# The first products of a decoder layer: two weights loaded in quarters, their products taken by inner tile in two banks, x loaded on GpSimd's queue, eight constant products in front instead of fourteen

## The chip, the core and the metric

The kernel runs on one core of a Trainium2 chip. The metric is the device time of one execution in microseconds; the time before is the median of three runs. The engines are named as the profile names them: PE is TensorE (matrix products), ACT is ScalarE, DVE is VectorE, POOL is GpSimd, SP is SyncE, which here only issues DMA transfers. PE, ACT, DVE, POOL and SP each work through their own instructions in a fixed order and wait on semaphores for one another. ACT, POOL and SP can each issue transfers; each has its own queue.

## The reference

One decoder layer on x, 1024 tokens by 1024 features, in float32: a SwiGLU feed-forward, a mixer (stick-breaking attention beside a Mamba-2 scan), cross-attention to 256 memory tokens, and a second SwiGLU, each between RMS norms. The change touches only the start of the first feed-forward:

```python
f = swiglu(rmsnorm(h, ffn1_pre_g[l]), ffn1_w_gu[l], ffn1_w_down[l])
h = h + 0.5 * rmsnorm(f, ffn1_post_g[l])

def swiglu(h, w_gu, w_down):
    gu = h @ w_gu
    g, u = jnp.split(gu, 2, axis=-1)
    return (jax.nn.silu(g) * u) @ w_down
```

The hidden width is 2816, 22 column tiles of 128 for the gate `g` and 22 for `u`.

## The kernel before

**Layout.** x is held transposed, features on the 128 partitions: 8 inner tiles (`d` or `k`, 0 to 7), each for two halves `hh` of the sequence, 512 tokens wide. An inner tile of one half is 128 x 512 floats, 256 KB. A weight tile is one column tile of 128 with all its 8 inner tiles, 128 x 8 x 128 floats, 512 KB.

**Precision.** Each float32 operand is split into a high part (rounded, by ScalarE) and a low part (the difference, by VectorE): `split` for weights (`whi`, `wlo`, from `wraw`), `scaled_split` for x times its gain (`xh`, `xl`, from the tiles `S`, which serve as landing place of x at the beginning). `mm3` then issues three products for one inner tile: high x high, high weight x low x, low weight x high x. So one column tile for one half takes 8 x 3 = 24 products of 512 columns, accumulated in one PSUM bank.

**The norm.** The products are made on x times gain, without the norm's factor. The factor of each token is found beside them: squares on ScalarE, sums on VectorE (`sumsq`, tile `acc`), a small product with ones (`rms_cols`, 4 products of one column, tile `ms`), root and reciprocal (`cpre`), and 4 products with the identity that lay the factor out as a row (`rms_rows`), copied to `rpre`. `gate` multiplies a finished bank by `rpre` and takes SiLU (tile `ft`); `up` multiplies the result by the other bank. Until `rpre` is there, a bank cannot be freed. Tag `mm` has three banks, tag `dn` four.

**The first stage.** `up_phase` begins with constant products (`warm`: ones x ones into `ms`, the result is not used). Then for weights 0, 1, 2 (gate 0, up 0, gate 1) it makes the weight tile (`wtile`: load, split) and after each calls `begin(i)`: x of half 0, then constants and the norm of half 0, then x and norm of half 1. The products follow in the order gate 0, up 0, gate 1 on half 0, then the same on half 1, then the weights 3, 4, 5 from a stream. The first three column tiles (`f` = 0 to 2) are done so; from f = 3 on (`seven`) the products run in a seven-product scheme on combined blocks, whose sums are made on VectorE and GpSimd (`wc`, `sq`, `e`, `S`).

**What sets the order.** TensorE's order is the order of the program: each product is tied behind the one before (`_pe`). A clock of estimated costs is kept beside (`self.clock`); `pinned(t)` places the norm's small products behind the first product at which that clock passes `t`. The other engines' orders come from a scheduler, except for instructions under `kp` while `inlater` holds, which keep the program's order, and `urgent`, which raises a priority. In the first two steps `inlater` holds. A pool's tag with `bufs=n` has n slots; the next tile of the tag waits until the oldest is free: `wraw` has 2 (each 512 KB of weight), `whi` and `wlo` 3 each, `raw2` 2.

## Time and profile before

| | us |
|---|---|
| median of 3 runs | 2595.53 |
| lowest, highest | 2594.32, 2598.31 |
| profiled execution, its own time | 2597.14 |
| span of that execution | 2595.4 |
| busy in the span: PE, DVE, ACT, POOL | 2573.2, 1989.8, 1290.5, 575.4 |

How to read the rows: a timeline row has start and duration in us, the engine, the line of the program, the operation, the tiles written and read (buffer numbers left out), the shape and the number of instructions merged into the row; in brackets the time that the engine sat idle before, and what ended it. `SPq` and `POOL DMA_DIRECT2D` rows are the issue of a transfer, not the transfer. A row of the DMA view names a transfer, its size and the time from issue to landing. A row by form gives the duration of one in ns as minimum, median and maximum. Products overlap in TensorE, so a product's duration is longer than the step from one to the next; the pace is read from starts.

### The profile page before, as it was taken

The page shows a single profiled execution, that of the slowest core. Times are in us where ns is not written, and L with a number is a line of the kernel's source. Part 1 is how long each engine was busy: PE and PEld are TensorE (multiplying, and loading weights), DVE is VectorE, ACT ScalarE, POOL GpSimd, SP SyncE. Part 2 cuts the span into 40 slices and gives each one's busy share as a digit, 9 for nine tenths or more (in the row PEclk, how much of TensorE's full clock was granted, in tenths as well). Part 3 has the DMA queues.
Part 4 walks back from the last instruction along what each step waited for, and adds up shares of the span by engine and source line. Part 5 has one row for each costly group of instructions (what it writes and reads, how often), then busy time and mean ns, then how long its engine had stood idle before and what let it go on. Part 6 is the DMA issues. An engine that isn't in the chain of part 4 may idle for free.

```text
span 2595.4 us, 36790 instructions
## 1 busy us (share of the span) xinstructions
PE 2573.2 (99%) x12850; PEld 2148.3 (83%) x12850; DVE 1989.8 (77%) x3049; ACT 1290.5 (50%) x2301; POOL 575.4 (22%) x668
## 2 busy tenths in 40 slices
PE   9999999999999999999999999999999999999999
PEld 7888888887787888888888898888878888888887
DVE  7888997779689884777777777876656888767767
ACT  7434444555356663555555554445554433334544
POOL 2555553001000001111111110101011655542000
PEclk9999999999999999999999999999999999999999
DMA  6448888655565516555554556547658453327554
GB/s 244 157 178 296 307 291 312 206 184 178 216 209 193 183 70 226 160 150 145 150 155 131 157 173 206 206 162 251 202 179 304 143 179 102 112 84 239 183 175 154
DMA packets 216042, 489.82 MB, mean 189 GB/s; under 512 B 26544, under 2 KB 35120, under 8 KB 215856
## 3 DMA queue, kind: packets, MB, share of 16 engines
q1 hardware_dynamic: 169232, 381.02, 45.0%
q0 software_dynamic: 22720, 62.93, 8.1%
q10 hardware_dynamic: 23904, 43.53, 4.5%
q8 instruction: 101, 1.65, 0.3%
q14 instruction: 85, 0.70, 0.1%
HBM read 327.46 MB, written 138.94 MB: 180 GB/s over the span
## 4 chain that ended last, share of the span: by engine, by line
PE 88%; DVE 4%; issue 1%; DMA 1%; ACT 1%; POOL 0%; DVEq 0%; ACTq 0%; POOLq 0%
PE mm L139 46%; PE dn L139 33%; PE z L139 2%; PE tr L142 2%; PE ms L142 1%; PE y L139 1%; PE ms L139 1%; PE seg L139 1%; PE st L139 0%; DVE wlo L263 0%; DMA wraw<-xs 0%; DVE hl L263 0%; DMA oraw<-mix 0%; PE mm L142 0%; DMA raw<-xs 0%
## 5 line engine op out<-in xcount | busy, mean ns | idle before, releaser
L139 PE MATMUL mm<-xh,whi 128*128 128x512 f32 x1312 | 519.7, 405 | 2.0 <-ACT sq L1806 1.4
L139 PE MATMUL mm<-xh,wlo 128*128 128x512 f32 x1280 | 491.5, 392 | 0.0
L139 PE MATMUL mm<-xl,whi 128*128 128x512 f32 (+1 forms) x1248 | 485.2, 389 | 0.3 <-DVE xl L270 0.3
L139 PEld LDWEIGHTS mm<-xh,wlo 128*128 128x128 f32 x1280 | 240.3, 188 | 52.4 <-DVE wlo L263 0.4
L139 PEld LDWEIGHTS mm<-xh,whi 128*128 128x128 f32 x1312 | 246.8, 188 | 44.1 <-issue 3.9
L139 PEld LDWEIGHTS mm<-xl,whi 128*128 128x128 f32 x1248 | 235.4, 189 | 34.1 <-DVE xl L270 1.0
L1792 DVE TENSOR_TENSOR_SCAN nb<-nb,begin 128x128 f32<-128x128 f32 (+7 forms) x128 | 171.5, 1351 | 41.9 <-ACT nb L1788 40.7
L1788 ACT ACTIVATE nb<-z,scale 128x128 f32<-128x128 f32 (+2 forms) x192 | 108.2, 580 | 70.7 <-PE z L139 70.2
L263 DVE TENSOR_TENSOR wlo<-wraw,whi 128x1024 fp32r<-128x1024 f32 x70 | 85.4, 1220 | 51.6 <-ACT whi L261 48.2
L261 ACT CAST whi<-wraw 128x1024 fp32r<-128x1024 f32 (+1 forms) x86 | 83.5, 970 | 73.8 <-PE mm L139 51.7
L1809 POOL DMA_DIRECT2D mix<-sq x64 | 52.8, 825 | 251.0 <-DVE sq L1807 190.5
L658 ACT ACTIVATE ft<-ft 128x512 f32<-128x512 f32 x88 | 55.5, 632 | 95.4 <-DVE ft L657 94.8
L139 PE MATMUL dn<-xh,wlo 128*128 128x512 f32 x296 | 101.2, 389 | 0.0
L761 POOL TENSOR_TENSOR wc<-raw,wraw 128x512 f32<-128x512 f32 x55 | 81.1, 1474 | 56.0 <-DVE wlo L263 23.3
L263 DVE TENSOR_TENSOR atl<-tr,ath 128x512 fp32r<-128x512 f32 (+1 forms) x107 | 67.3, 630 | 32.2 <-ACT ath L261 31.8
L761 POOL TENSOR_TENSOR wc<-wraw,raw 128x512 f32<-128x512 f32 x56 | 78.6, 1404 | 52.2 <-DVE whi L263 16.5
L261 ACT CAST ath<-tr 128x512 fp32r<-128x512 f32 (+1 forms) x107 | 58.3, 545 | 58.8 <-PE tr L142 55.6
L858 POOL TENSOR_TENSOR ft<-ft,e 128x512 f32<-128x512 f32 x37 | 59.8, 1616 | 124.4 <-DVE e L854 56.5
L139 PE MATMUL mm<-ath,v 128*128 128x256 f32 x320 | 84.6, 287 | 0.7 <-ACT sq L1806 0.5
L139 PE MATMUL dn<-xh,blk 128*128 128x512 f32 x264 | 85.2, 389 | 0.0
L139 PE MATMUL mm<-atl,v 128*128 128x256 f32 x320 | 83.1, 282 | 0.7 <-DVE atl L263 0.7
L261 ACT CAST wlo<-wc 128x512 fp32r<-128x512 f32 x79 | 49.1, 621 | 68.6 <-PE dn L139 22.1
(582 smaller groups left out, 6770.9 us busy)
## 6 DMA issues: line engine op xcount, KB each, us to landing
whi<-dwhi SPq DMA_DIRECT2D x82, 512.0 KB, 3.7
wlo<-dwlo SPq DMA_DIRECT2D x82, 512.0 KB, 5.0
wraw<-in_w_gu SPq DMA_DIRECT2D x43, 512.0 KB, 4.2
dwhi<-bh SPq DMA_DIRECT2D x78, 256.0 KB, 4.1
dwlo<-bl SPq DMA_DIRECT2D x78, 256.0 KB, 4.0
raw<-in_w_gu SPq DMA_DIRECT2D x37, 512.0 KB, 4.1
wraw<-xs SPq DMA_DIRECT2D x56, 256.0 KB, 3.0
xs<-ft ACTq DMA_DIRECT2D x54, 256.0 KB, 3.0
```

Source lines behind the costliest of these rows:

```text
L139: self._pe(self.nc.tensor.matmul(out, lhsT, rhs, start=start, stop=stop, skip_group_check=self.more), cost)
L142: self._pe(self.nc.tensor.transpose(out, src, self.ident if ident is None else ident), 109.0)
L261: self.kp(self.nc.scalar.copy(hi, src))
L263: self.nc.vector.tensor_tensor(out=lo, in0=src, in1=hi.bitcast(F32), op=ALU.subtract)
L658: nc.scalar.activation(t, t, AF.Silu)
L761: inst = (nc.vector if early else nc.gpsimd).tensor_tensor(out=t, in0=a, in1=b, op=op)
L858: nc.gpsimd.tensor_tensor(out=t1, in0=t1, in1=e, op=ALU.mult)
L1788: nc.scalar.activation(nb[:, s0:s1], z[:, 0:n], AF.Sigmoid, scale=sc[:, i : i + 1])
L1792: nc.vector.tensor_tensor_scan(out=nb[:, 0:Wd][:, ::-1], data0=nb[:, 0:Wd][:, ::-1], data1=begin[:, S - Wd : S][:, ::-1], initial=0.0, op0 ...
L1809: nc.gpsimd.dma_start(out=self.mix_d[p][a * 64 : a * 64 + 64, csl], in_=o, accum_op=ALU.add)
```

## The change

Weights 0 and 1 get their landing tiles and split tiles at once, and each is loaded in four transfers, two inner tiles (128 KB) each, alternating between the two weights, on SP's queue. Tile 0 of x for half 0 follows the first quarter on the same queue; the other 15 tiles of x (both halves) are issued on GpSimd's queue, where before four were. The parameters are issued on ScalarE's queue, not on SP's. The splits of the quarters stand between those of x in the program's order. Weight 2 lands in a slot of `raw2` instead of `wraw`. The products of weights 0 and 1 on half 0 run side by side: for each inner tile three products of the one into one bank, three of the other into a second, both of tag `dn` (before: all of weight 0 into a bank of `mm`, then all of weight 1). The norm's small products of half 0 are pinned at 17500 and 21000 instead of 8500 and 13500; those of half 1 stay at 24000 and 27500. `warm` makes 8 constant products instead of 14.

```diff
-            first = []
-            begin(-1)
-            for i in range(3):
-                self.inlater = i < 2
-                first.append(self.wtile(wgu[i]))
-                begin(i)
-                self.inlater = False
+            begin.warm()
+            first, raws = [], []
+            for i in range(2):
+                raws.append(self.t(self.wp, [P, KT, P], F32, "wraw", bufs=2))
+                first.append([self.t(self.wp, [P, KT, P], F32R, n, bufs=3) for n in ("whi", "wlo")])
+            quarters = [(i, slice(2 * n, 2 * n + 2)) for n in range(4) for i in range(2)]
+            for n, (i, q) in enumerate(quarters):
+                self.tc.keep_in_program_order(nc.sync.dma_start(out=raws[i][:, q], in_=wgu[i][:, q]))
+                if n == 0:
+                    begin.load(0, 0, nc.sync)
+            for d in range(1, 2 * KT):
+                begin.load(d // KT, d % KT, nc.gpsimd)
+            self.inlater = True
+            for n, (i, q) in enumerate(quarters):
+                self.split(*(x[:, q] for x in first[i]), raws[i][:, q])
+                if n < 2:
+                    begin.split(0, n)
+                elif n % 2:
+                    begin.split(0, n - 1)
+                    begin.split(0, n)
+            begin.behind()
+            raw = self.t(rw, [P, KT, P], F32, "raw2", bufs=2)
+            self.tc.keep_in_program_order(nc.sync.dma_start(out=raw, in_=wgu[2]))
+            first.append([self.t(self.wp, [P, KT, P], F32R, n, bufs=3) for n in ("whi", "wlo")])
+            self.split(*first[2], raw)
+            begin.consts()
+            begin.norm(0, 17500, 21000)
+            self.inlater = False
+            for d in range(KT):
+                begin.split(1, d)
+            begin.norm(1, 24000, 27500)
...
-            ts = []
-            for hh in range(2):
-                up(0, hh, gate(first[0], hh), first[1])
-                ts.append(gate(first[2], hh))
+            ps = [self.t(self.dnp, [P, H], F32, "dn", bufs=4) for _ in range(2)]
+            for k in range(KT):
+                for (wh, wl), x in zip(first, ps):
+                    self.mm3(x, [(wh[:, k, :], wl[:, k, :], self.XH[0][k], self.XL[0][k])], k == 0, k == KT - 1)
+            t = ft()
+            with self.urgent():
+                scaled(t, ps[0], 0)
+                nc.vector.tensor_tensor(out=t, in0=t, in1=ps[1], op=ALU.mult)
+            store(0, 0, t)
+            ts = [gate(first[2], 0)]
+            up(0, 1, gate(first[0], 1), first[1])
+            ts.append(gate(first[2], 1))
...
-            nc.sync.dma_start(out=self.params, in_=ap["params"])
+            nc.scalar.dma_start(out=self.params, in_=ap["params"])
...
-                for _ in range(14):
+                for _ in range(8):
```

Three places show how the instructions move. First TensorE's beginning; `whi_215` and `whi_246` are weights 0 and 1 before, `whi_208` and `whi_211` after, `xh_4` and `xh_5` the high parts of inner tiles 0 and 1. Before:

```order
L139 MATMUL ms_198<-onesr_115 128x512 x14
L139 MATMUL mm_376<-xh_4_80,whi_215 128x512
L139 MATMUL mm_376<-xl_20_96,whi_215 128x512
L139 MATMUL mm_376<-xh_4_80,wlo_216 128x512
L139 MATMUL mm_376<-xh_5_81,whi_215 128x512
L139 MATMUL mm_376<-xl_21_97,whi_215 128x512
```

and with the change:

```order
L140 MATMUL ms_198<-onesr_115 128x512 x8
L140 MATMUL dn_388<-xh_4_80,whi_208 128x512
L140 MATMUL dn_388<-xl_20_96,whi_208 128x512
L140 MATMUL dn_388<-xh_4_80,wlo_209 128x512
L140 MATMUL dn_389<-xh_4_80,whi_211 128x512
L140 MATMUL dn_389<-xl_20_96,whi_211 128x512
L140 MATMUL dn_389<-xh_4_80,wlo_212 128x512
L140 MATMUL dn_388<-xh_5_81,whi_208 128x512
```

Each inner tile of x now feeds six products instead of three before the next tile is asked for, and both weights are needed from the start.

Second, ScalarE around the two norms; `sq_105` to `sq_111` are squares of half 1, `whi_675` is the fourth weight (its slot is weight 0's), `rpre_101` the factor of half 0. With the change:

```order
L335 ACTIVATE cpre_100_305<-ms_307,small_114 128x4
L360 ACTIVATE acc_104_336<-S_73_189 128x512
L363 ACTIVATE sq_107_344<-S_74_190 128x512
L363 ACTIVATE sq_108_347<-S_75_191 128x512
L363 ACTIVATE sq_109_350<-S_75_191 128x512
L262 CAST whi_675<-wraw_673 128x1024
L363 ACTIVATE sq_110_353<-S_76_192 128x512
L350 COPY rpre_101_306<-ms_314 128x512
L363 ACTIVATE sq_111_356<-S_76_192 128x512
```

Before, the fourth weight's CAST stood 13 instructions behind the row's copy; now it stands two ahead of it.

Third, VectorE in the first of the seven-product tiles (f = 3), where `e_184` gathers a difference of products and the other rows are low parts of weights and of x. Before:

```order
L730 SCALAR_TENSOR_TENSOR cb_892<-cb_892,params_78,cb_893 128x512
L263 TENSOR_TENSOR xl_28_104<-braw_815,xh_12_88 128x512
L263 TENSOR_TENSOR wlo_976<-wc_974,wlo_976 128x512
L827 TENSOR_TENSOR e_184<-sq_270_950,dn_998 128x512
L263 TENSOR_TENSOR xl_29_105<-rpost_835,xh_13_89 128x512
```

and with the change:

```order
L755 SCALAR_TENSOR_TENSOR cb_904<-cb_904,params_78,cb_905 128x512
L264 TENSOR_TENSOR xl_28_104<-braw_827,xh_12_88 128x512
L852 TENSOR_TENSOR e_184<-sq_270_962,dn_1010 128x512
L264 TENSOR_TENSOR wlo_988<-wc_986,wlo_988 128x512
L264 TENSOR_TENSOR xl_29_105<-rpost_847,xh_13_89 128x512
```

The difference `e` now goes one place earlier, ahead of a weight's low part. From about the second seven-product tile (f = 4) on, the order on every engine is the same as before.

More of the change, by code (lines that the diff above doesn't have):

```diff
@@ L1 @@
 from contextlib import ExitStack, contextmanager
+from types import SimpleNamespace
 import numpy as np
@@ L2273, in consts, with load_x, split_x, behind @@
                     nc.vector.tensor_scalar(out=g, in0=g, scalar1=0.5, scalar2=None, op0=ALU.mult)
-            def load_x(hh):
-                order = self.tc.keep_in_program_order
-                for d in range(KT):
-                    x, eng = self.F[hh][d], (nc.sync, nc.gpsimd)[d % 2 if hh == 0 else 0]
-                    order(eng.dma_start(out=x, in_=ap["xT"][d, :, hh * H : (hh + 1) * H]))
-                    self.scaled_split(self.XH[hh][d], self.XL[hh][d], x, self.par("ffn1_pre_g", d))
-                if hh == 0:
-                    order(nc.gpsimd.tensor_copy(small[:, 4:5], self.XH[0][6][:, 0:1].bitcast(F32)))
+            order = self.tc.keep_in_program_order
+            def load_x(hh, d, eng):
+                order(eng.dma_start(out=self.F[hh][d], in_=ap["xT"][d, :, hh * H : (hh + 1) * H]))
+            def split_x(hh, d):
+                self.scaled_split(self.XH[hh][d], self.XL[hh][d], self.F[hh][d], self.par("ffn1_pre_g", d))
+            def behind():
+                order(nc.gpsimd.tensor_copy(small[:, 4:5], self.XH[0][6][:, 0:1].bitcast(F32)))
             def warm():
@@ L2296, in norm_x @@
                 self.pre(hh, accs, t1, t2)
-            def begin(step):
-                if step < 0:
-                    warm()
-                elif step == 0:
-                    load_x(0)
-                elif step == 1:
-                    consts()
-                    norm_x(0, 8500, 13500)
-                else:
-                    load_x(1)
-                    norm_x(1, 24000, 27500)
+            begin = SimpleNamespace(
+                warm=warm, load=load_x, split=split_x, behind=behind, consts=consts, norm=norm_x,
+            )
             self.kv_d = [[tc.dram_tile([P, 4, MEM], F32R, name=f"kv{h}{n}") for n in range(2)] for h in range(4)]
```

## The prediction

> **What bounds the kernel now.** First the page, busy time by engine.
>
> ```profile
> PE 2573.2 (99%) x12850; PEld 2148.3 (83%) x12850; DVE 1989.8 (77%) x3049; ACT 1290.5 (50%) x2301; POOL 575.4 (22%) x668
> ```
>
> TensorE is busy for 2573.2 of 2595.4 us: only 22 us in the whole kernel are idle. So the second view is TensorE's timeline of the beginning (start and duration in us, in brackets the idle time before and what ended it), with a line of the chain for the pace of undisturbed products. The page counts the constant products `ms<-onesr` as work; here they are part of the loss.
>
> ```profile
> 1.10 6.18 PE L139 MATMUL ms<-onesr 128*128 128x512 f32 x14 [1.10 <-POOL onesr L2265]
> 7.50 0.50 PE L139 MATMUL mm<-xh,whi 128*128 128x512 f32 x1 [0.22 <-ACT xh L268]
> 8.29 0.50 PE L139 MATMUL mm<-xl,whi 128*128 128x512 f32 x1 [0.30 <-DVE xl L270]
> ...
> 23.21 1.02 PE L139 MATMUL ms<-small,acc 128*128 128x1 f32 x8 [0.22 <-DVE acc L363]
> 24.09 0.48 PE L139 MATMUL mm<-xh,wlo 128*128 128x512 f32 x1
> ...
> 25.57 1.06 PE L139 MATMUL ms<-ident,cpre 128*128 128x128 f32 x8
> 26.38 0.47 PE L139 MATMUL mm<-xh,wlo 128*128 128x512 f32 x1
> ...
> 28.02 0.50 PE L139 MATMUL mm<-xh,whi 128*128 128x512 f32 x1 [0.47 <-DVE ft L657]
> 116.22 2.72 PE dn L139 x12
> ```
>
> An undisturbed product takes 2.72 / 12 = 0.2267 us. The first useful one starts at 7.50, and the first one on the second half of the sequence (hh = 1) at 28.02. Between them lie 72 products (3 weights x 8 inner tiles x 3), 16.32 us, and the small products of the first norm, (24.09 - 23.21) + (26.38 - 25.57) = 1.69 us. The rest, 28.02 - 7.50 - 16.32 - 1.69 = 2.51 us, is lost in waits. Without the norm, which moves, the second half starts at 28.02 - 1.69 = **26.33 us**: that is the number to beat. From there on TensorE is full up to 90 us (stretches: length, then busy time of each engine), so what is won by then is kept at least so far.
>
> ```profile
> 28.00:52.00 24.00, 23.98 (x113) 20.11 (x114) 17.55 (x26) 17.31 (x25) 2.12 (x4) 1.00 0.35 122
> 52.00:90.00 38.00, 38.00 (x168) 31.16 (x166) 31.71 (x42) 23.45 (x40) 19.66 (x27) 1.00 0.68 228
> ```
>
> **The first product.** Before, it waits for tile 0 of x, which stands on SP's queue behind 512 KB of weight.
>
> ```profile
> 1.19 0.42 SPq L185 DMA_DIRECT2D wraw<-in_w_gu  x1
> 1.66 2.10 SPq L2279 DMA_DIRECT2D S<-in_xT  x4
> wraw<-in_w_gu SPq DMA_DIRECT2D x1, 512.0 KB, 4.1
> S<-in_xT SPq DMA_DIRECT2D x1, 256.0 KB, 5.0
> 6.72 2.56 ACT L268 ACTIVATE xh<-S,params 128x512 fp32r<-128x512 f32 x4 [0.40 <-DMA S<-in_xT]
> 7.50 2.73 DVE L270 SCALAR_TENSOR_TENSOR xl<-S,params,xh 128x512 fp32r<-128x512 f32 x4
> 0.00:2.00 2.00, 1.00 0.11 18
> 2.00:3.00 1.00, 1.00 0.96 190
> 3.00:4.00 1.00, 1.00 0.96 324
> 4.00:5.00 1.00, 1.00 0.98 354
> 5.00:6.00 1.00, 1.00 1.00 332
> 6.00:7.00 1.00, 1.00 1.03 375
> 7.00:8.00 1.00, 1.00 1.04 416
> 8.00:9.00 1.00, 1.00 1.03 404
> 9.00:10.00 1.00, 1.00 1.06 395
> ```
>
> The last rows are stretches: length, granted clock, DMA share, GB/s. Tile 0 landed at 1.66 + 5.0 = 6.66 us, and the first product followed 0.84 us later. Adding the rates up, 1.48 MB had moved by 6.66; parameters, weight and tile 0 are 0.89 MB of that, so GpSimd's tiles beside them multiplied the wait by 1.66. Now only parameters, a quarter weight and tile 0 stand ahead, 0.50 MB. Alone they would be down at 3.9 us; with as much again on GpSimd's queue at 5.3; at the measured 1.66, 0.83 MB, at 4.8 us. I take 4.8: the first product starts at 4.8 + 0.84 = **5.64 us**, the second, behind the subtraction on VectorE, another 0.79 later (8.29 - 7.50), at **6.43**.
>
> **The 71 products from there** take 16.1 us at full pace, to 22.5 us, if three supplies keep up. *Data:* per inner tile TensorE needs 6 x 0.2267 = 1.36 us. At 38% of the traffic (0.66 / 1.66 = 40% is the most that GpSimd's queue can have had before) tile 4 lands at 9.8 us, its two parts are ready 0.7 + 0.7 us later, at 11.3, and the products ask for them from 11.6 on; tile 5 is ready at 13.0 and asked for at 13.0; tiles 6 and 7 have more room, because SP's queue runs dry at about 11.3 (2.07 MB at 62%). The parameters on ScalarE's queue cost it an issue ahead of its first table load, at a time when it has nothing to do: free. *Splitting:* the quarters cost more instructions.
>
> ```profile
> L261 ACT CAST whi<-wraw x6: 1038/1042/1055, 5.3 to 46.5; 128x1024 fp32r<-128x1024 f32 x6
> L263 DVE TENSOR_TENSOR wlo<-wraw,whi x6: 1218/1224/1225, 6.4 to 47.7; 128x1024 fp32r<-128x1024 f32 x6
> L261 ACT CAST blk<-wraw x1: 618/618/618, 55.7 to 55.7; 128x512 fp32r<-128x512 f32 x1
> L263 DVE TENSOR_TENSOR blk<-wraw,blk x1: 685/685/685, 56.4 to 56.4; 128x512 fp32r<-128x512 f32 x1
> ```
>
> Carrying the step from 1024 to 512 elements on to 256 gives 0.41 us on ScalarE and 0.42 on VectorE. Two inner tiles need 2 x (0.41 + 0.64) = 2.1 us on ScalarE (2.56 / 4 for x) and 2 x (0.42 + 0.68) = 2.2 on VectorE (2.73 / 4), under TensorE's 2.72: hidden. The third weight lands near 11.3, its split ends by 15.6, and it is first asked for at 17.1. *Pace:* this is the term that decides.
>
> ```profile
> L139 PE MATMUL ms<-onesr x7: 470/628/628, 4.2 to 6.8; 128*128 128x512 f32 x7
> ```
>
> The fourteen constant products run at (6.8 - 1.1) / 13 = 0.438 us each, half pace, though the granted clock stands at 1.00; only the last is shorter (0.470), and the useful ones are fast. So it took about 5.7 us of products to reach full pace. Eight of them last 3.5 us, to 4.6; then TensorE sits for 1 us. What is left to run slowly I bound from both sides: 14 - 8 = 6 products if the break costs nothing, 14 if it starts the count afresh. Each slow product costs 0.438 - 0.227 = 0.211 us. I take the middle, ten, 2.1 us, since the break is of the size neither to be ignored nor to count as a stop; that also gives the tiles 4 to 7 room. The second half then starts at 22.5 + 2.1 = **24.6 us** (23.8 to 25.5). Gain: 26.33 - 24.6 = **1.7 us** (0.8 to 2.5).
>
> [...]
>
> **What follows.** The inputs of the second half land by about 21 us (7 MB in all at the rates above) and are needed from 24.6 on. The first norm now sits at the 81st product; on VectorE a split of 1.2, seven sums and four splits of x at about 0.67 each stand before it from 14.4 on, so its sum is ready near 23 us and asked for at 26.6: free. The second norm is tight. ScalarE takes the fourth weight's CAST ahead of the first norm's row copy, and that CAST waits until product 96 frees its slot. Behind it: 1.04 on ScalarE, then on VectorE 1.1 for the split, two scalings and two sums at about 0.6 each: 4.7 us. TensorE has 19 products and a norm's row, 19 x 0.2267 + 0.81 = 5.1 us less the tail of product 96, 4.9. I cost it at nothing; if late, at most 1 us. The third weight sits in a `raw2` slot, so one of GpSimd's later loads of x (L674) waits for its split near 15.6; in ScalarE's order the first use of these loads comes behind the first norm's row and SiLU, ten microseconds and more later: free. The three banks of `mm` hold, because the first two products now lie in `dn`: the wait of 0.47 us at 28.02 is part of the 2.51 us that go.
>
> Further on only VectorE's order moves, and there the first of two waits is met:
>
> ```profile
> 90.32 3.00 PE L139 MATMUL dn<-S,whi 128*128 128x512 f32 x12 [0.30 <-DVE e L827]
> ...
> 113.21 3.01 PE L139 MATMUL mm<-S,wlo 128*128 128x512 f32 x12 [0.85 <-DVE e L827]
> ```
>
> The difference `e` now goes ahead of a split of 0.685 us, so this 0.3 us should go. The 0.85 us wait before 113 us hangs on GpSimd's chain, whose order is unchanged: kept.
>
> **Sum:** 1.7 + 0.3 = 2.0 us. The profiled execution took 2597.14 us (span 2595.4 and 1.7 around it), 1.6 above the median of the runs, 2595.53. So 2595.1 for such an execution and **2593.5 us** for the median.
>
> **Rivals.**
> *Full pace at once* (0.18). Against it stand the thirteen slow products; for it, that products were fast at 8.29 right after a 0.2 us wait. Then the second half starts at 22.5: gain 3.8 + 0.3 = 4.1, **2591.4 us**.
> *The gain is given back* (0.20). For it: POOL's chain and the waits at 90 and 113 us, and later phases that wait for DMA; against: every later order is unchanged and TensorE drives it. Then **2595.5**, within the runs' own 4 us.
> *Slower: the quarters arrive late* (0.08). The 128 KB of constants took 7.9 us to land in the traffic and the 105 KB of parameters 2.1 almost alone:
>
> ```profile
> rpost<-in_consts SPq DMA_DIRECT2D x1, 128.0 KB, 7.9
> params<-in_params SPq DMA_DIRECT2D x1, 105.0 KB, 2.1
> ```
>
> If a quarter cannot go faster than 128 / 105 x 2.1 = 2.6 us and they do not overlap, the last pair lands at about 2 + 8 x 2.6 + 0.7 (tile 0) = 23.5 us; with 1.4 us of splitting and 36 products (8.2 us) behind it the second half starts at 33.1, a loss of 6.8: **2602.3**. It decides once the last pair lands after 26.33 - 9.6 = 16.7 us; I expect 8 to 10, since the transfers before overlapped at a DMA share of 1.0. [...]
> The forecast itself has 0.54.
>
> **Range and chances.** The best case, 4.1 with the wait before 113 us gone too, gives 2590.6; the runs' own spread takes that to 2590.0. A start that brings nothing, with the second norm late by 1 us and a spread of 1, gives 2597.5. The forecast alone is 2592.5 to 2594.5. What this kernel can be told from no change by is about 0.2%, 5.2 us: below 2590.3 is faster, above 2600.7 slower. The forecast and the second rival lie inside; the first mostly too. Faster 0.12, same 0.80, slower 0.08.
>
> **What would show it.** The first `dn` product at 5.6 us, not 7.5; constant products ending near 4.6 and a gap of 1 us; about ten products 0.44 apart, then 0.227; no wait for a quarter after the second inner tile; the second half at 24.6; no wait at the product fed by the second norm; the wait for `e` near 88 us gone. I am wrong if the products stay slow past 12 us, if a tile of x on GpSimd's queue is what TensorE waits for, or if the 2 us seen at 25 us are not there at 2595.

## The result, and the profile after

The changed kernel takes 2601.28 us (median of 22 runs, 2597.48 to 2605.10) against 2596.10 for the kernel before (22 runs on the same chip, 2594.31 to 2600.39). The ratio is 1.0018, with a 95% interval of 1.0012 to 1.0023: 5 us slower, where 2 us faster was forecast. The profiled execution took 2604.58 us (span 2602.8), 3.3 above its median.

The timeline of TensorE answers to the rows of before (start, duration, in brackets the idle time before and its releaser). From 8.13 to 29.29 us no row has a wait.

```profile
PE 2576.7 (99%) x12844; PEld 2150.1 (83%) x12844; DVE 1992.8 (77%) x3055; ACT 1293.1 (50%) x2307; POOL 583.0 (22%) x679
1.10 3.78 PE L140 MATMUL ms<-onesr 128*128 128x512 f32 x8 [1.10 <-POOL onesr L2298]
5.41 0.80 PE L140 MATMUL dn<-xh,whi 128*128 128x512 f32 x1 [0.54 <-ACT xh L269]
6.20 0.80 PE L140 MATMUL dn<-xl,whi 128*128 128x512 f32 x1
...
8.13 0.80 PE L140 MATMUL dn<-xh,whi 128*128 128x512 f32 x1 [0.70 <-ACT whi L262]
...
12.56 0.55 PE L140 MATMUL dn<-xl,whi 128*128 128x512 f32 x1
12.95 0.39 PE L140 MATMUL dn<-xh,wlo 128*128 128x512 f32 x1
...
26.15 0.39 PE L140 MATMUL mm<-xh,whi 128*128 128x512 f32 x1
...
29.29 1.02 PE L140 MATMUL ms<-small,acc 128*128 128x1 f32 x8 [0.94 <-DVE acc L364]
...
39.49 1.05 PE L140 MATMUL ms<-small,acc 128*128 128x1 f32 x8 [0.39 <-DVE acc L364]
...
92.69 2.97 PE L140 MATMUL dn<-S,whi 128*128 128x512 f32 x12 [1.02 <-ACT blk L262]
...
117.43 4.42 PE L140 MATMUL mm<-S,wlo 128*128 128x512 f32 x12 [2.04 <-DVE e L852]
...
480.74 7.23 PE L140 MATMUL dn<-hl,dx 128*128 128x512 f32 x24 [2.33 <-ACT F L1130]
```

The start works: the first product stands at 5.41 us instead of 7.50. Then it is lost step by step. Fourteen products run at half pace, to 12.56 (0.63 and 0.80 us long, 0.39 from 12.95 on). The second half starts at 26.15, where 26.33 was to beat. The sums of both norms come late. TensorE reaches the seven-product scheme 1.65 us behind the kernel before (the same product at 46 us), and there the waits before 93 and 117 us, 0.30 and 0.85 before, are 1.02 and 2.04. A part of the loss is in no wait. Stretches of the change (length; busy time of PE, PEld, DVE, ACT and POOL; granted clock, DMA share, GB/s):

```profile
118.00:119.00 1.00, 1.00 (x5) 0.86 (x4) 1.00 (x3) 0.54 (x1) 0.00 (x0) 0.85 0.30 61
119.00:122.00 3.00, 3.00 (x8) 2.30 (x7) 2.65 (x6) 0.69 (x2) 1.66 (x2) 0.50 0.85 325
```

Right behind the long wait the granted clock is half for 3.41 us, in which TensorE does half the work (8 products from 119 to 122 us, 15 in the same stretch of `halves` at 1.00): 1.7 us. The same follows the wait before 480.74 (0.50 from 481 to 483). At the 500th product the change is 5.87 us behind, at the last one 7.5; 3.4 of that are these two windows. A third one, at 658 us (0.50 from 659 to 661), has its like in the kernel before, at 648 us (0.50 from 649 to 652).

### The profile page after: what moved, and what is told of

Same layout as the page of the kernel before. It is cut to its first block, busy times and chain, and to the rows that moved or that the text cites. A ratio compares the mean times of both kernels' runs of the same rounds, so it can differ in the third digit from the quotient of the medians.

```text
span 2602.8 us, 36804 instructions
## 1 busy us (share of the span) xinstructions
PE 2576.7 (99%) x12844; PEld 2150.1 (83%) x12844; DVE 1992.8 (77%) x3055; ACT 1293.1 (50%) x2307; POOL 583.0 (22%) x679
## 3 DMA queue, kind: packets, MB, share of 16 engines
q8 instruction: 101, 1.65, 0.3%
## 5 line engine op out<-in xcount | busy, mean ns | idle before, releaser
L140 PE MATMUL mm<-xh,whi 128*128 128x512 f32 x1296 | 513.1, 405 | 1.5 <-ACT sq L1839 1.5
L140 PE MATMUL mm<-xh,wlo 128*128 128x512 f32 x1264 | 484.8, 391 | 0.0
L140 PE MATMUL mm<-xl,whi 128*128 128x512 f32 (+1 forms) x1232 | 478.7, 389 | 0.0
L264 DVE TENSOR_TENSOR wlo<-wraw,whi 128x1024 fp32r<-128x1024 f32 (+1 forms) x75 | 85.2, 1136 | 50.8 <-ACT whi L262 50.2
L262 ACT CAST whi<-wraw 128x1024 fp32r<-128x1024 f32 (+2 forms) x91 | 83.5, 918 | 77.7 <-PE mm L140 51.3
L140 PE MATMUL dn<-xh,wlo 128*128 128x512 f32 x312 | 108.3, 392 | 0.0
L140 PE MATMUL dn<-xh,whi 128*128 128x512 f32 x256 | 91.0, 397 | 1.6 <-ACT whi L262 0.7
L786 POOL TENSOR_TENSOR wc<-wraw,raw 128x512 f32<-128x512 f32 x56 | 79.6, 1421 | 53.7 <-DVE blk L264 16.7
L262 ACT CAST whi<-wc 128x512 fp32r<-128x512 f32 x81 | 50.2, 620 | 68.5 <-PE dn L140 24.4
```

Of the source, the lines that this page charges most:

```text
L140: self._pe(self.nc.tensor.matmul(out, lhsT, rhs, start=start, stop=stop, skip_group_check=self.more), cost)
L262: self.kp(self.nc.scalar.copy(hi, src))
L264: self.nc.vector.tensor_tensor(out=lo, in0=src, in1=hi.bitcast(F32), op=ALU.subtract)
L786: inst = (nc.vector if early else nc.gpsimd).tensor_tensor(out=t, in0=a, in1=b, op=op)
```

## The experiments

Each kernel was timed in 11 runs beside 33 of the kernel before (four kernels share each set of 33), so that ratios compare and medians of different sets do so only roughly. The table has what each left: the ratio to before, how far TensorE is behind the kernel before (+) or ahead of it (-), in us, at the product that stands at 46 us there and at the one that stands at 129 us, and the waits before 93 and 117 us.

| kernel | ratio (95%) | at 46 us | at 129 us | wait 93 | wait 117 |
|---|---|---|---|---|---|
| the change | 1.0018 (1.0012 to 1.0023) | +1.65 | +5.87 | 1.02 | 2.04 |
| warm14 | 1.0015 (1.0007 to 1.0024) | +1.54 | +6.21 | 1.52 | 2.03 |
| halves | 1.0016 (1.0007 to 1.0025) | +0.48 | +4.38 | 2.36 | 2.05 |
| x1_sp | 1.0009 (1.0000 to 1.0018) | +0.15 | +3.57 | 1.87 | 2.05 |
| early_sq | 1.0015 (1.0007 to 1.0024) | +0.64 | +3.73 | 1.56 | 2.05 |
| sq_pins | 1.0005 (0.9996 to 1.0014) | +1.28 | +1.31 | 0.30 | 0.85 |
| halves_pins | 1.0016 (1.0007 to 1.0025) | -0.04 | +2.58 | 0.91 | 2.04 |
| halves_pins_w14 | 0.9994 (0.9985 to 1.0003) | -0.02 | -0.19 | none | 1.19 |
| actq | 1.0009 (1.0000 to 1.0018) | -0.05 | +4.05 | 0.92 | 2.06 |
| halves_pins_kept | 1.0016 (1.0007 to 1.0025) | -0.06 | +4.68 | 3.43 | 0.71 |
| actq_kept | 0.9998 (0.9989 to 1.0007) | -0.69 | +1.94 | 1.48 | 2.01 |
| sq_pins_h14 | 0.9993 (0.9984 to 1.0002) | +1.06 | +1.03 | 0.30 | 0.85 |
| best_k | 1.0006 (0.9998 to 1.0015) | -0.34 | +1.81 | 2.81 | 0.49 |
| after_silu | 1.0007 (0.9998 to 1.0016) | +0.87 | +0.85 | none | 1.40 |
| halves_pins_silu | 0.9998 (0.9989 to 1.0007) | -0.73 | -0.64 | none | 1.39 |
| before8 | 1.0006 (0.9997 to 1.0015) | +0.62 | +0.63 | 0.31 | 0.86 |
| h14_late | 1.0002 (0.9993 to 1.0011) | +0.12 | +5.02 | 1.73 | 2.01 |

### Pace: warm14 and before8

`warm14` is the change with one number back; by the traces each engine's order is that of the change:

```diff
-                for _ in range(8):
+                for _ in range(14):
```

> The change with fourteen constant products again. Theory P (slow products eat the gain): the fourteen slow useful products (5.41 to 12.56 us) become fast from about 8 us on; then only the last quarter of weight 1 binds (ScalarE casts it at 16.18, product 39 can follow near 17.3), and product 72 starts at 25.3 to 25.5 us instead of 26.15: 0.7 us won there. Theory O (ScalarE's order makes the norms and the sums late): product 72 may move, but the wait for the first norm's sum grows from 0.94 by as much, and from 41 us on nothing is won: median within 1 us of the change, 2601.3.

TensorE's timeline of that kernel:

```profile
1.10 5.98 PE L140 MATMUL ms<-onesr 128*128 128x512 f32 x14 [1.10 <-POOL onesr L2298]
6.92 0.39 PE L140 MATMUL dn<-xh,whi 128*128 128x512 f32 x1
...
8.35 0.50 PE L140 MATMUL dn<-xh,whi 128*128 128x512 f32 x1 [0.58 <-ACT whi L262]
...
29.14 1.02 PE L140 MATMUL ms<-small,acc 128*128 128x1 f32 x8 [0.91 <-DVE acc L364]
```

Not one useful product is slow, yet weight 1's first quarter holds the fourth at 8.35, later pieces hold later ones (the 38th starts at 17.95, 0.53 us behind the one before it), and the second half starts at 26.03 instead of 26.15. The wait for the norm's sum is as long as in the change, 0.91 against 0.94, and so is the time, 2601.54 us. In the change, the slow products hide behind late data; the pace was not what cost the gain.

`before8` is the kernel before with eight constant products instead of fourteen; here too the orders are the same.

> The kernel before with eight constant products instead of fourteen and nothing else; ScalarE's order stays as it was. Theory P, measured alone: the first products of x start at 7.5 us as before (x's tile lands at 6.7 us), full pace comes after 11 us instead of 7, 10 to 18 products run slowly at 0.21 us each; what of it the waits of the start (2.5 us) do not absorb stays to the end: product 72 at 28.5 to 31 us, median 0.5 to 3 us above before. If the pace costs nothing here either: product 72 at 28.0 to 28.4, no difference.

A row of its timeline and one of its stretches:

```profile
7.75 0.50 PE L139 MATMUL mm<-xh,whi 128*128 128x512 f32 x1 [2.87 <-ACT xh L268]
9.00:11.00 2.00, 2.00 (x6) 1.52 (x6) 1.82 (x4) 1.65 (x3) 0.00 (x0) 0.50 1.02 403
```

Behind the 2.87 us without work the granted clock is half, to 11.6 us (0.50 from 9 to 11, 0.71 from 11 to 12). In the end this start loses 0.62 us, since waits of before take up the rest. The waits before 93 and 117 us are those of before, and the ratio cannot be told from 1. So by this trace the pace alone is worth about half a microsecond; the interval of the ratio leaves room for up to 0.15%.

### The queues: halves and x1_sp

`halves` loads the two weights in pieces of 256 KB; the splits stay in quarters.

```diff
+            halves = [(i, slice(4 * n, 4 * n + 4)) for n in range(2) for i in range(2)]
-            for n, (i, q) in enumerate(quarters):
+            for n, (i, q) in enumerate(halves):
```

> The change with weights 0 and 1 loaded in halves of 256 KB (2 KB in a row) instead of quarters (1 KB in a row); the splits stay in quarters. Theory D (the two queues take turns by packet, so SP's small packets get a small share of the bytes: 8 to 12 us it moved 363 packets of 0.33 MB, GpSimd's queue 331 of 1.09 MB): SP's share rises, the last piece of a weight lands at 12 to 14 us instead of 16.2, the third weight at 15 to 17 instead of 18.7; the wait of 0.94 at 29.3 us goes and the median falls by 1 to 3 us. Theory P alone: landings may move, but product 72 stays at 26 us or later and the median within 1 us of the change.

The transfers of 8 to 12 us by queue (q0 is GpSimd's, q1 SP's; packets, MB, share of the engines), of the change and then of `halves`:

```profile
q0 software_dynamic: 331, 1.09, 74.8%
q1 hardware_dynamic: 363, 0.33, 25.5%
```

```profile
q0 software_dynamic: 267, 0.88, 58.9%
q1 hardware_dynamic: 268, 0.68, 44.7%
```

In both stretches the queues move about equally many packets (331 and 363, 267 and 268). Of the bytes, SP's queue got 23% with rows of 1 KB (0.33 of 1.42 MB) and 44% with rows of 2 KB (0.68 of 1.56 MB). From 12 to 17 us of the change it is so too (383 and 387), from 2 to 8 us it is not (247 and 710), so the turns of the expectation hold for these stretches alone. In the change, ScalarE's timeline shows what waits for SP's queue:

```profile
7.67 0.40 ACT L262 CAST whi<-wraw 128x256 fp32r<-128x256 f32 x1 [2.31 <-DMA wraw<-in_w_gu]
...
16.18 0.41 ACT L262 CAST whi<-wraw 128x256 fp32r<-128x256 f32 x1 [1.16 <-DMA wraw<-in_w_gu]
...
18.68 1.05 ACT L262 CAST whi<-raw 128x1024 fp32r<-128x1024 f32 x1 [0.85 <-DMA raw<-in_w_gu]
20.20 0.30 ACT L2303 COPY ident<-rpost 128x128 f32<-128x128 f32 x1 [0.47 <-DMA rpost<-in_consts]
```

With halves the last piece is cast at 12.94 and the third weight at 14.96, without waiting, and the norms' waits are gone. At 46 us 1.2 us are won against the change. The wait for weight 1's first piece at 8 us stays (0.93 us, 0.70 in the change); twice as much is loaded before it. But the waits before 93 and 117 us grow by about what was won, and the time is 2600.12 us, no better.

`x1_sp` issues x's second half on SP's queue behind the third weight and the constants, as before the change.

```diff
-            for d in range(1, 2 * KT):
-                begin.load(d // KT, d % KT, nc.gpsimd)
+            for d in range(1, KT):
+                begin.load(0, d, nc.gpsimd)
...
             for d in range(KT):
+                begin.load(1, d, nc.sync)
                 begin.split(1, d)
```

> The change with the eight tiles of x for the second half issued on SP's queue behind the third weight and the constants, as before the change, so that GpSimd's queue has seven tiles. Theory D: GpSimd's queue is done near 9 us, the last quarter lands at 11 to 12 us instead of 16.2, the third weight near 14.5, ScalarE's squares start near 16 instead of 20.6; product 72 at 24.5 to 25.3 us; the waits of 0.94 and 0.39 at the norms go, those before 93 and 117 us fall back to 0.3 and 0.85; median 2595 to 2598. Theory P: product 72 at 26 us, median 2600 or more.

The third weight is cast at 16.34 instead of 18.68, both waits for norms are gone, TensorE is within 0.15 us of before at 46 us. The second half still starts at 26.37: behind the eight constant products thirteen are slow here (0.63 and 0.80 us long), and the first quarter of weight 1 is waited for 1.18 us. The ratio falls to 1.0009 (its interval still overlaps that of the change), but the waits at 93 and 117 us stand at 1.87 and 2.05. So late data explain the start, and not the larger loss behind it.

### ScalarE's order: early_sq, sq_pins

In `early_sq` the squares and sums of the first half stand behind the splits of their own tiles, not behind the third weight and the constants.

```diff
                 elif n % 2:
                     begin.split(0, n - 1)
                     begin.split(0, n)
+                if n % 2:
+                    begin.square(0, n - 1)
+                    begin.square(0, n)
...
-                accs = self.new_accs()
-                for d in range(KT):
+                accs = early[0] if hh == 0 else self.new_accs()
+                for d in range(KT if hh else 0):
```

> The change with the squares and sums of the first half put behind the splits of their own two inner tiles in the program's order, not behind the third weight and the constants. Theory O: the norm's sum is ready near 21 us instead of 30, the waits of 0.94 (29.3 us) and 0.39 (39.5 us) go; ScalarE and VectorE reach the sums of the seven-product scheme 3 to 5 us earlier, the waits before 93 and 117 us fall from 1.02 and 2.04 to about 0.3 and 0.85, and the half-clock window at 118.7 us goes with the long wait: product 500 some 3 to 5 us earlier than in the change, median 2596 to 2598.5. Theories P and D without O: product 72 stays at 26.1 us, only the 1.3 us of the two norms are won and are lost again at 93 and 117 us: median 2600 to 2601.5.

The sum is ready at 20.55 us, 8.6 us earlier, and the norms' waits are gone. But the factor's row is still copied at 34.97, because its products are pinned behind product 98, and GpSimd's fetch behind it comes only 1 us earlier, at 46.18. `sq_pins` moves the pins too:

```diff
-            begin.norm(0, 17500, 21000)
+            begin.norm(0, 11000, 14000)
```

> The kernel with the early squares, and in addition the first norm's small products pinned at 11000 and 14000 instead of 17500 and 21000 (behind products 51 and 65 instead of 81 and 98). Theory N (the pin: since the row of the first norm's factor now stands behind product 98, ScalarE copies it at 35 to 36 us instead of 26.7, and everything behind it in ScalarE's and VectorE's order, SiLU, scaling of the fetched x, the sums of the seven-product scheme, comes some 9 us later, which TensorE meets as waits before 93 and 117 us): the copy moves to about 26.5 us, GpSimd's fetch that stood at 46 us back to 37 to 40, the waits of 1.56 and 2.05 us fall to 0.3 and 0.85 (before's), product 500 at 129 to 130 us instead of 132.5, median 2597 to 2598.5. Without N (the late sums have another cause): the waits stay within 0.3 us, median 2600.5 to 2602.5.

TensorE's rows at the two waits, of `early_sq` and then of `sq_pins`:

```profile
92.22 2.97 PE L140 MATMUL dn<-S,whi 128*128 128x512 f32 x12 [1.56 <-ACT blk L262]
...
116.94 3.01 PE L140 MATMUL mm<-S,wlo 128*128 128x512 f32 x12 [2.05 <-DVE e L855]
```

```profile
91.60 2.98 PE L140 MATMUL dn<-S,whi 128*128 128x512 f32 x12 [0.30 <-DVE e L855]
114.48 3.06 PE L140 MATMUL mm<-S,wlo 128*128 128x512 f32 x12 [0.85 <-DVE e L855]
```

The copy moved to 28.03, GpSimd's fetch to 39.80, and both waits have the very values of before. Its start is 1.28 us behind before, and 1.31 us is all it is behind at 129 us; the ratio fell from 1.0015 to 1.0005, the median from 2601.62 to 2597.25. The two intervals overlap; it is the rows that show the effect.

### One instruction tied: halves_pins, halves_pins_w14, after_silu, halves_pins_silu

The same edit of the pins on `halves`, whose sum is ready later:

```diff
-            begin.norm(0, 17500, 21000)
+            begin.norm(0, 13500, 16000)
```

> The kernel with the weights in halves, and in addition the first norm pinned at 13500 and 16000 (behind products 62 and 74). The sum is ready at 24.8 us there, so the pin costs TensorE at most 0.4 us. Theory N: the row is copied at about 28 us instead of 34.83, the waits of 2.36 and 2.05 us before 93 and 117 us fall to 0.3 to 0.6 and 0.85 to 1.2; product 500 at 129.5 to 130.5 instead of 133.1, median 2597 to 2599. Without N: waits stay, median 2600.

This one missed: the copy moved from 34.83 to 29.05, and the wait before 93 us fell from 2.36 to 0.91 (0.3 to 0.6 expected), but the one before 117 us stayed at 2.04 and the ratio at 1.0016. Its twin has fourteen constant products (`range(14)` again) and was meant as a test of pace:

> The same with fourteen constant products. Halves let the weights land by 12 us, so now the pace can show, if it costs anything: theory P: no slow product after 8.5 us, product 72 some 1 to 2 us earlier than with eight (24.8 to 25.8), and with the pin right this lasts to the end: median 1 to 1.5 us below that of eight. Theory D: data still bind (the first quarter of weight 1 at 8 us, then ScalarE's splits): product 72 within 0.5 us of the run with eight.

From 47 to 84 us the twins are within 0.05 us of each other on TensorE (the twin is 1.46 us ahead at product 60, and a wait of 1.33 us for the norm's sum takes that back). At 129 us they are 2.77 us apart, in the median 5 us. The programs differ by six constant products and by swapped places in the scheduled orders: by the traces about five on TensorE, seven on ScalarE, fourteen on VectorE and one on GpSimd. One of these, on ScalarE, of `halves_pins` and then of its twin:

```profile
44.94 0.59 ACT L350 COPY rpre<-ms 128x512 f32<-128x512 f32 x1 [2.97 <-PE ms L140]
46.09 1.05 ACT L262 CAST whi<-wraw 128x1024 fp32r<-128x1024 f32 x1 [0.57 <-PE mm L140]
47.16 1.28 ACT L684 ACT_TABLE_LOAD   x1
48.45 0.63 ACT L684 ACTIVATE ft<-ft 128x512 f32<-128x512 f32 x1
```

```profile
44.90 0.59 ACT L350 COPY rpre<-ms 128x512 f32<-128x512 f32 x1 [2.79 <-PE ms L140]
45.50 1.28 ACT L684 ACT_TABLE_LOAD   x1
46.80 0.63 ACT L684 ACTIVATE ft<-ft 128x512 f32<-128x512 f32 x1
...
49.08 1.03 ACT L262 CAST whi<-wraw 128x1024 fp32r<-128x1024 f32 x1
```

The CAST of the sixth weight waits until TensorE has used the third, which gives it its slot. Where it stands ahead of the SiLU, SiLU and the scaling of the fetched x wait with it. The kernel before has it behind; with it the factor's row and GpSimd's first combined weight there:

```profile
26.66 0.59 ACT L349 COPY rpre<-ms 128x512 f32<-128x512 f32 x1 [0.45 <-PE ms L139]
...
44.77 0.63 ACT L658 ACTIVATE ft<-ft 128x512 f32<-128x512 f32 x1
...
46.54 1.04 ACT L261 CAST whi<-wraw 128x1024 fp32r<-128x1024 f32 x1
...
69.77 1.30 POOL L761 TENSOR_TENSOR wc<-wraw,raw 128x512 f32<-128x512 f32 x1
```

The change has it ahead, with the longest wait:

```profile
36.02 0.57 ACT L350 COPY rpre<-ms 128x512 f32<-128x512 f32 x1
...
44.98 0.59 ACT L350 COPY rpre<-ms 128x512 f32<-128x512 f32 x1
47.97 1.05 ACT L262 CAST whi<-wraw 128x1024 fp32r<-128x1024 f32 x1 [2.40 <-PE mm L140]
...
49.56 1.28 ACT L683 ACT_TABLE_LOAD   x1
50.85 0.63 ACT L683 ACTIVATE ft<-ft 128x512 f32<-128x512 f32 x1
...
73.23 1.30 POOL L786 TENSOR_TENSOR wc<-wraw,raw 128x512 f32<-128x512 f32 x1
```

`after_silu` is the change with that one CAST tied behind that SiLU, by an edge without a semaphore:

```diff
-        self.kp(self.nc.scalar.copy(hi, src))
+        i = self.nc.scalar.copy(hi, src)
+        self.kp(i)
+        if getattr(self, "mark", False):
+            self._after(i.ins, self.silu.ins)
```

(`mark` holds while the sixth weight's tile is made, `silu` is the first SiLU of the second half.)

> The change with one instruction moved on ScalarE: the CAST of the sixth weight (47.97 us, 2.40 us of waiting for TensorE in front of it) is tied behind the first SiLU of the second half (50.85 us); loads, pins, constant products and the start as in the change. Theory S (this CAST, which waits for TensorE to free its slot, holds up SiLU and the scaling of the fetched x behind it, and with them the sums of the seven-product scheme): SiLU starts at 46.5 to 47.5 us, the waits of 1.02 and 2.04 us before 93 and 117 us fall to 0.3 to 0.6 and 0.85 to 1.3, product 500 at 130.5 to 132.5 instead of 134.6, median 2597 to 2599.5 instead of 2601.3. Without S: waits within 0.3 us of the change's, median 2600.5 to 2602.

Its rows, of ScalarE, of TensorE and of GpSimd:

```profile
47.84 0.63 ACT L688 ACTIVATE ft<-ft 128x512 f32<-128x512 f32 x1
50.13 1.03 ACT L262 CAST whi<-wraw 128x1024 fp32r<-128x1024 f32 x1
114.05 3.02 PE L140 MATMUL mm<-S,wlo 128*128 128x512 f32 x12 [1.40 <-DVE e L859]
71.23 1.30 POOL L793 TENSOR_TENSOR wc<-wraw,raw 128x512 f32<-128x512 f32 x1
```

SiLU starts 3.0 us earlier, GpSimd's first `wc` 2.0 us earlier (0.8 of each is the start's), the wait at 93 us is gone, the one at 117 us is 1.40 (0.85 to 1.3 expected), and no half-clock window follows it (the next twelve products take 3.02 us, 4.42 in the change). At 129 us the kernel is 0.85 us behind before instead of 5.87, of which 0.78 had been gone by 46 us, by another course of the start. The ratio is 1.0007 instead of 1.0018.

The tie moves more than that CAST, since the scheduler places what stands behind it anew. TensorE's order is the same, but by the traces some six instructions of ScalarE, fourteen of VectorE and one of GpSimd change places up to 125 us. Two of these stand in the chain that TensorE waits for, on VectorE the first `e` and on GpSimd a product `ft`. In the change and then in `after_silu`:

```profile
91.87 0.68 DVE L852 TENSOR_TENSOR e<-sq,dn 128x512 f32<-128x512 f32 x1
110.05 1.28 POOL L883 TENSOR_TENSOR ft<-ft,e 128x512 f32<-128x512 f32 x1
```

```profile
88.85 0.68 DVE L859 TENSOR_TENSOR e<-sq,dn 128x512 f32<-128x512 f32 x1
105.44 1.29 POOL L890 TENSOR_TENSOR ft<-ft,e 128x512 f32<-128x512 f32 x1 [1.27 <-ACT ft L688]
```

The first `e` follows 0.47 us behind the end of GpSimd's `sq` instead of 2.84, and `ft` stands two `wc` earlier, so that the next `sq`, on which the wait at 117 us hangs, starts at 111.56 instead of 114.94.

`halves_pins_silu` does the same to `halves_pins`:

> The kernel with halves and early pins and eight constant products (2600.64 us), with the same one instruction tied behind SiLU; its twin with fourteen constant products (2595.68) has that order by itself and reaches 84 us within 0.05 us of it. Theory S: waits before 93 and 117 us from 0.91 and 2.04 to 0 to 0.3 and 1.15, product 500 at 128.3 to 129.3 instead of 131.3, median 2595.5 to 2598. Without S (the number of constant products itself matters, or run to run phase of the clock): 131 and 2600.

Here too: no wait at 93 us, 1.39 at 117 us, ratio 0.9998 instead of 1.0016. So with the constant products as they were, one instruction tied and the orders that follow from it, two kernels win 0.11% and 0.18%, 2.9 and 4.7 us by the ratios, each known to about 0.1%. What the CAST's own place is worth without the other swaps is not shown. The profiled execution of the second is 0.73 us ahead at 46 us by luck: its products run at full pace from 6.89 us on (0.39 us long), those of `halves_pins` from 12.72.

### What that does not explain: halves_pins_kept, actq, actq_kept, h14_late, best_k

`actq` puts weight 1's halves on ScalarE's queue, x's second half on SP's, has fourteen constant products, called behind these loads in the program, and the pins at 14500 and 17000. The main lines of the edit:

```diff
-                self.tc.keep_in_program_order(nc.sync.dma_start(out=raws[i][:, q], in_=wgu[i][:, q]))
+                eng = (nc.sync, nc.scalar)[i]
+                self.tc.keep_in_program_order(eng.dma_start(out=raws[i][:, q], in_=wgu[i][:, q]))
...
-            begin.norm(0, 17500, 21000)
+            begin.norm(0, 14500, 17000)
```

> Everything that the traces name, together: weight 0 in halves on SP's queue, weight 1 in halves on ScalarE's queue, the second half of x on SP behind the third weight and the constants, fourteen constant products, the first norm pinned at 14500 and 17000. If D, P and N are the causes: weight 1's first half lands before 6.5 us, no wait over 0.5 us from the first product at 7.4 on, product 72 at 23.9 to 25 us, the waits before 93 and 117 us at 0.3 and 0.85: 1.5 to 2.5 us faster than the kernel before, 2594.5 to 2596. If something else is behind the loss: no faster than the kernel before, 2597 or more.

The start is the best so far (the fourth product at 7.47, nothing slow), 0.84 us ahead of before at product 60; then it waits 1.8 us for the norm's sum. It has SiLU ahead of the CAST, and still waits of 0.92 and 2.06 us. The other two places are those of the change: `e` comes 2.84 us behind the end of `sq`, and `ft` at 108.25, behind the two `wc`. A second place in ScalarE's order was suspected: the CAST of a combined weight behind a copy (`sq`) that waits for TensorE. Two kernels keep these in the program's order:

```diff
+                keep, self.inlater = self.inlater, self.inlater or bool(begin and f == first_seven)
                 self.split(w[:, 0], w[:, 1], a)
+                self.inlater = keep
...
-                nc.scalar.copy(t5, a)
+                i = nc.scalar.copy(t5, a)
+            if begin and f == first_seven:
+                self.tc.keep_in_program_order(i)
```

> The kernel with halves and the first norm's pins at 13500 and 16000, and in addition the splits of the first combined weights and the first copy of a bank (sq) kept in the program's order, so that on ScalarE the CAST of the low half of a combined weight stands before the copy that waits for TensorE (81.99 us, idle 3.09), as it does in the kernel before and in the one with early squares and early pins. Theory F (this place in ScalarE's order makes the waits before 93 and 117 us): the CAST moves from 82.47 to about 79 us, the waits of 0.91 and 2.04 us fall to 0.3 and 0.85 or less, the half-clock window can go with them; median 2597 to 2598.5 instead of 2600.6. Without F (the chain behind is late as a whole): waits within 0.4 us of what they were, median 2600 or more.

> The kernel with weight 1 on ScalarE's queue and the rest of the repairs, with the same two orders kept. Theory F: the CAST moves from 82.33 to about 80 us, the wait of 2.1 us before 117 us falls to 0.85 or less, product 500 from 132.8 to 128 to 129.5 us, median 2595 to 2596.5 instead of 2599.2. Without F: 2599.

That theory fell: in the first the wait at 93 us grew to 3.43 while the one at 117 us fell to 0.71, ratio unchanged; in the second they stood at 1.48 and 2.01, and it took 2598.33 us. Of the 2.1 us that the second wins at 129 us, 0.6 are a better start and most of the rest is a half-clock window that `actq` had and this execution did not (the twelve products behind the wait took 4.42 and 3.01 us). Keeping these orders did bring the first `e` to 0.47 us behind `sq`, in both; that alone does not remove the wait at 93 us. `best_k` is `actq_kept` with the squares one pair of tiles behind the splits and the pins at 12500 and 14500:

```diff
+                if n in (3, 5):
+                    begin.square(0, n - 3)
+                    begin.square(0, n - 2)
...
             self.split(*first[2], raw)
+            for d in range(4, KT):
+                begin.square(0, d)
...
-            begin.norm(0, 14500, 17000)
+            begin.norm(0, 12500, 14500)
```

> All repairs together: weight 1 in halves on ScalarE's queue, x's second half on SP, fourteen constant products, the squares of the first half one pair of tiles behind the splits, the first norm at 12500 and 14500, and the two orders kept. Product 72 at 25.5 to 26.5 us with the norm in front of it (before: 28.02), no wait over 0.5 us for a norm's sum, the waits before 93 and 117 us at 0.3 and 0.85: 1.5 to 2.5 us faster than before, 2594 to 2595.5. If the sums of the seven-product scheme depend on more than ScalarE's order: a gain at 40 us that is given back by 117 us, 2596 to 2598.

Ahead by 0.34 us at 46 us, 1.81 behind at 129 us, waits 2.81 and 0.49: the second of the two cases expected, with a median of 2599.27 us, above the 2596 to 2598 given for it. `h14_late` is `halves_pins_w14` with other pins:

```diff
-            begin.norm(0, 13500, 16000)
+            begin.norm(0, 15000, 17500)
```

> The kernel with halves, fourteen constant products and the first norm pinned at 15000 and 17500 instead of 13500 and 16000, where its twin waits 1.3 us for the norm's sum. The wait goes (0 to 0.3 us) and product 81 comes 1 us earlier, at 29.1 us. If TensorE's own gains last: product 500 at 127.6, median 2594.5 to 2595. If the sums of the seven-product scheme set the pace by 117 us: the 1 us is taken back there, product 500 at 128.5 or later, median 2595.5 or more.

The later pins did not even win the wait for the norm (1.0 us is left), and shifted the scheduled orders of ScalarE again: waits of 1.73 and 2.01, 5.2 us lost at 129 us against its twin, and a ratio of 1.0002 against 0.9994. The CAST stands behind SiLU here too, but `e` comes 2.83 us behind `sq` and `ft` at 109.23, behind the two `wc`. The three kernels that have all three places, `halves_pins_w14`, `after_silu` and `halves_pins_silu`, are those with no wait at 93 us and 1.2 to 1.4 us at 117 us. No run moves one of these places alone, so what each is worth stays open.

### Toward a faster kernel: sq_pins_h14

`sq_pins` with the loads of `halves` and `range(14)` for the constant products.

> The kernel with early squares and early pins (2597.25 us, its start 1.28 us behind the kernel before), and in addition the weights in halves and fourteen constant products. If pace and landing times are all that its start lacks, product 72 moves from 29.46 to 27 us or less (its two norm products included), 1.5 to 2.5 us, and since ScalarE's order stays as it was, the gain lasts: median 2595 to 2596. If the early squares themselves hold up the splits: product 72 at 28 us or more, median 2596.5 to 2597.5.

With the waits of before and a start 1.06 us behind, it takes 2595.69 us, ratio 0.9993, as in the first case expected, while its start is that of the second; `halves_pins_w14` takes 2595.68, ratio 0.9994. Both intervals hold 1. The second half starts only at 29.23 in the former, against 28.02 before: the squares between the splits hold up VectorE's low parts, so that TensorE waits four times for `xl`. No kernel of the study is faster than before by more than the measurement can tell.

## Why the prediction was wrong

**The first product** (5.64 and 6.43 forecast) came at 5.41 and 6.20: right.

**Data.** "At 38% of the traffic" for GpSimd's queue failed. It got 77% (1.09 of 1.42 MB) from 8 to 12 us. The 38% was taken from a kernel in which SP's rows were long (0.71 of 1.99 MB for GpSimd's queue from 2 to 8 us, 36%); the change shortened them to 1 KB and put nearly four times as many tiles on the other queue. The quarters, expected down at 8 to 10 us, were cast until 16.2, the third weight at 18.68 instead of 11.3. From the second on they took 6.0 to 11.0 us from issue to landing. The rival of late quarters had its threshold at 16.7 us and came within 0.6 us of it: the last quarter was down at about 16.15. In `warm14`, where no product is slow, the second half starts at 26.03, so late data and the waits that follow from them take nearly the whole gain by themselves.

**Pace.** Fourteen slow products, to 12.56 us, where ten were taken and 14 was the upper bound. But it is not a term to add: `warm14` removes all fourteen and starts the second half 0.12 us earlier. Two limits stood side by side, and the sum took each as if it were the only one.

**The second half at 24.6 us** came at 26.15: of the gain of 1.7 us 0.18 was there.

**The norms.** "The first norm is free" failed by 0.94 us and "tight, at most 1 us" for the second came out at 0.39. Both follow from the step on data, since the squares stand behind the third weight and the constants in ScalarE's order: VectorE's sums, expected from 14.4 us on, began at 21.8.

**"Free" for ScalarE's order** is, of the steps that the prediction took, the one with the largest error. The prediction looked at GpSimd's loads and the first norm's row and said that what stands behind is ten microseconds later and free. It looked at the place of the fourth weight's CAST, not at the sixth's, which now stands ahead of SiLU. It kept the 0.85 us wait, because the order of GpSimd's chain is unchanged, and expected the 0.3 to go, because `e` moves ahead of a split. GpSimd's order is indeed unchanged there; but what feeds it comes later, since the rows behind the norm moved with it: the row of the factor from 26.66 to 36.02, the fetch of x from 38.07 to 47.23, the first combined weight from 69.77 to 73.23. TensorE meets that chain at 93 and 117 us. In the sum the two waits were to shrink from 1.15 to 0.85 us; they grew to 3.06. `after_silu`, its one tie and the swaps behind it, takes back some 0.11% of the 0.18%, with 0.1% of uncertainty, and by its trace all of the two waits' growth but 0.25 us; `sq_pins` shows that an early sum with early pins restores both waits to their values. That the waits behind 46 us come from the orders and from a late first norm is shown; which of the places that `after_silu` has and `actq` and `h14_late` lack does it stays open.

**What was in no step:** the half-clock windows, which the sum put at nothing without a word. Each costs 1.7 us (3.41 us at 0.50), and the profiled execution of the change has two more than before's. That is no accident of this execution: the mean granted clock on record is 0.9977 over the 22 runs of the change, and 0.9990 to 0.9993 over each of the four sets of 33 runs of the kernel before. By these figures, which are rounded to 0.001 in each run and count nothing ahead of the first rise (the records have 1.00 from 6 to 12 us of the change, where the products are slow), an execution of the change loses an estimated 0.13 to 0.16% of 2600 us of clock more, 3.4 to 4.2 us, or two such windows. Where TensorE has work in them, they are a large part of the 5 us.

Of the rivals, "the gain is given back" named the places, GpSimd's chain and the waits at 90 and 113 us, and was too kind: it let the chain take what the start had won, and no more. The slower one had the late quarters right and their end wrong: it has them too slow one by one, where the other queue's traffic made them late, and the second half at 33.1 us, where it came at 26.15. That its 2602.3 us lies within 1.1 us of the median is luck.

## What to carry to other kernels

When a change moves a small product that releases a chain of other engines, follow that chain through the static order of each engine, and price a place behind an instruction that waits for the bound engine: an engine that is 50% busy, as ScalarE here, can still be late. Work out a queue's share anew when the size of its rows changes: here it went from 23% to 44% of the bytes with rows of 2 KB for 1 KB. Where two supplies are close to their limits, the later one counts; removing one of them alone brings nothing (0.12 us at the second half in `warm14`). And a tie put into a scheduled program to move one instruction can move others: compare the orders before giving the effect to that one.

## What the runs showed of the hardware that was not expected

**Where TensorE's clock fell.** Between the first rise of the clock and the program's last steps, the granted clock of the change is half in three stretches of 3.41 us, from 118.71, 480.52 and 658.01 us, and that of the kernel before in one, from 648.68. By the timelines TensorE had been idle for 2.04, 2.11 and 1.42 us of the 3.41 us ahead of the three, and for 1.84 us ahead of the one. Behind the waits of 1.63 us before 474.17 (kernel before) and of 1.53 us before 1441.33 (change) the clock stayed at 1.00. Of the nine profiles with a wait of 2.01 to 2.06 us before 117 us, four have slow products behind it (the next twelve took 4.36 to 4.55 us), five have not (3.01 to 3.04 us). `halves` is one of the five, with 2.05 us before 117.58:

```profile
116.00:119.00 3.00, 1.42 (x6) 1.20 (x7) 2.16 (x3) 0.62 (x1) 2.03 (x2) 1.00 0.40 141
```

So behind a wait of 2 us the next twelve products took some 1.4 us longer in four executions than in the other five; what decides between them is not shown. The runs of one kernel spread over 3 to 9 us, and by the author's estimate such losses may be part of why. The record agrees: in the four sets of the kernel before, runs with a mean clock of 1.000 took 2596.0 to 2596.7 us on average, runs with 0.998 took 2599.7 to 2600.1.

**When full pace came.** In the change and in six of its variants with eight constant products (`halves`, `x1_sp`, `early_sq`, `sq_pins`, `halves_pins`, `after_silu`) the first product of 0.39 or 0.40 us starts between 12.72 and 14.00 us; in `halves_pins_silu`, also with eight, products of that length stand from 6.89 us on. With fourteen constant products they stand from 6.33 (`halves_pins_w14`), 6.92 (`warm14`) and 7.24 us on (`actq`). What sets the moment is not shown. Between `halves_pins` and `halves_pins_silu`, whose orders are the same up to there, the eighth product of the third weight comes at 22.28 and 20.47 us: the kernel with the early full pace is 1.8 us ahead there, of which 0.31 was there at the fourth product (8.33 and 8.02).
